# Modulation of the opening computed in quarters instead of halves, in a transformer block kernel on Trainium2

## The chip, the cores and the metric

The kernel runs on one core of a Trainium2 chip. Its engines work side by side, each through its own list of instructions in order: TensorE (PE, matrix products and transpositions), VectorE (DVE), ScalarE (ACT), GpSimd (POOL) and SyncE (SP, which here only issues transfers). The metric is the time of one execution on the device in microseconds; 3 runs are known of the kernel before.

## The reference

One layer of a diffusion transformer over 2048 tokens of width 1024, with 256 context tokens. What the opening of the kernel has to do with:

```
mod_x = silu(c) @ w_mod + b_mod            # six vectors of 1024; the first two: shift sh1, scale sc1
mod_c = silu(c_ctx) @ w_mod + b_mod        # the same for the context tokens
h_x = rmsnorm(x, norm1_g) * (1 + sc1) + sh1
h_c = rmsnorm(ctx, norm1_g) * (1 + sc1c) + sh1c
p_x = h_x @ w_in                           # columns: k | v | q | u | vg | gate a | gate b
k_c, v_c = (h_c @ w_in[:, :256]) split     # keys and values of the context
... attention, gated mixing, branch merge, residual
... second norm, squared-ReLU MLP, residual
```

Everything is float32.

## The kernel before

`project` computes the input projection for two blocks of 1024 tokens. Each is a 2 x 2 block product (tokens in halves of 512, the inner width in halves of 512, columns in halves) done with seven products instead of eight. They come in the order `SUMS = (0, 1, 5, 6, 4, 2, 3)`. Product 0 has as its left operand `h[0]`, the first token half with inner half 0; product 1 has `h[1]`, the first token half with inner half 1. Products 5, 6, 4 have sums and differences that need the second token half (`x1` in the code) as well. `h_five` makes the operand of product 5 from the turned pieces of both halves.

A product has two chunks `c`, each of two 128-row pieces of the inner width. A float32 product is done as three matmuls of a faster format: each operand is split into a high part (a cast on ACT) and a low part (a subtraction on DVE), and `product` multiplies high by high, high by low, low by high (lines 1744, 1745, 1746). A chunk of the first pair of columns thus has 4 token tiles x 2 pieces x 3 = 24 matmuls of 384 columns. `pair_chunk` casts and splits the weights of one chunk (lines 712, 713); `ready` holds the chunks that are prepared.

The left operands must stand with the inner width on the partitions. So `turn` transposes four 128 x 128 tiles on PE (line 192, in `transposes`), and one ACT instruction (line 537) applies the modulation's scale `G1` and shift `S1` on the way out of PSUM. `operand` casts and splits the result (lines 572, 573). `h_scale` squares and sums x on ACT (line 515), takes the reciprocal root in small DVE steps (lines 163 to 179) and scales x on DVE (line 524).

`G1` and `S1` come from the modulation, which is done in halves of 512 columns (four pieces of 128). `mod_weights` loads 16 tiles of w_mod of 256 KB each; `mod_products` multiplies them with the silu of the two conditioning vectors, 32 columns wide (line 339); `mod_finish` copies the row out (line 348), transposes it (line 351) and adds bias and norm weight on DVE (lines 357, 361). The first half is done in `mod_head` before any product, the second by the generator `opening` between products 0 and 1.

`opening` is a generator with the work that goes between the products: `pairs_run` calls its hook twice a chunk, and each call runs `opening` to its next `yield`. It turns x1 (`raw_turned`), prepares product 5's operands and, with `opening_terms`, the weights of products 5, 6, 4 and 3. Those of 4 and 3 go to DRAM (`t_d`) and are loaded back for their product. From the hook's 20th call on (`CONTEXT_AT`) it runs `context_keys`, which turns the context tokens (line 999) and multiplies them.

The order of each engine comes from the framework's scheduler, within limits that the kernel writes down: for index ranges in `pins` the order written holds on all engines, in `fixed` on PE and DVE, in `loads` on SP. Each queue, those of DMA issues too, is worked through in order. PSUM has 4 banks named "a" for the products and 4 named "b" for all else.

Of the kernel before, what the change touches and what calls it, by code (L numbers as in the profile page):

```python
# [13 lines left out]
ALU = mybir.AluOpType  # L14
# [4 lines left out]
P = 128  # L19
D = 1024  # L20
KC = D // P
# [5 lines left out]
GROUPS = 8  # L27
# [40 lines left out]
CONTEXT_AT = 20  # L68
ON_VECTOR = (2, 4, 8, 14)
# [3 lines left out]
class Kern:  # L73
# [115 lines left out]

    def transposes(self, ps, srcs):  # L190
        for i, s in enumerate(srcs):
            self.nc.tensor.transpose(ps[:, i * P : (i + 1) * P], s, self.ident)  # L192
# [88 lines left out]
    def mod_head(self):  # L281
# [4 lines left out]
        at = 0  # L286
        for src, eng in (
            (I["c"][0], nc.sync),
            (I["c_ctx"], nc.sync),
            (I["b_mod"][0, : 2 * D], nc.scalar),  # L290
            (I["norm1_g"][0], nc.scalar),
        ):
            src = src.rearrange("(k p) -> k p", p=P)
            eng.dma_start(rows[at : at + src.shape[0]], src)
            at += src.shape[0]
        nc.scalar.dma_start(rows[at : at + GROUPS], I["gm_bs"][0])
        self.rope_consts()
        at += GROUPS
# [20 lines left out]
        w = self.mod_weights(0, "hx")  # L319
        self.h_scale(self.x0, dve=True)  # L320
        ps = self.bank([TB])
        for k in range(KC):
            self.mod_products(ps, w, k)
        self.mod_finish(ps, 0)

    def mod_weights(self, half, tag):
        w = []
        for k in range(KC):
            w.append([self.sb(tag, [TB]) for _ in range(2)])
            for i, t in enumerate(w[k]):  # L330
                lo = i * D + half * TB
                self.nc.sync.dma_start(
                    t, self.I["w_mod"][0, k * P : (k + 1) * P, lo : lo + TB]
                )
        return w

    def mod_products(self, ps, w, k):
        for i in range(2):
            self.nc.tensor.matmul(
                ps[32 * i : 32 * i + 32], self.wide[:, k, :], w[k][i],  # L340
                start=k == 0, stop=k == KC - 1,
            )

    def mod_finish(self, ps, half):
        nc = self.nc
        bcol, gcol = self.mod_cols
        row = self.t2([TB])
        nc.scalar.copy(row[:64], ps[:64])
        pt = self.bank([HK, 64])
        for j in range(HK):  # L350
# [3 lines left out]
        ks = slice(half * HK, (half + 1) * HK)  # L354
        for i, dst in enumerate((self.S1, self.G1)):
            bs = slice(i * KC + half * HK, i * KC + (half + 1) * HK)
            nc.vector.tensor_tensor(
                out=dst[:, ks], in0=pt[:, :, 32 * i : 32 * i + 2],
                in1=bcol[:, bs].unsqueeze(2).broadcast_to([P, HK, 2]), op=ALU.add,
# [3 lines left out]
            in1=gcol[:, ks].unsqueeze(2).broadcast_to([P, HK, 2]),  # L363
# [352 lines left out]
    def pairs_run(self, pairs, h, ready, hook, direct):  # L716
# [246 lines left out]
    def context_keys(self):  # L963
# [8 lines left out]
        for k0 in range(0, KC + 2, 2):  # L972
# [19 lines left out]
            if k0 < KC:  # L992
# [3 lines left out]
                tmp = self.t2([2, CTX])  # L996
                for j in range(2):
# [114 lines left out]
    def project(self, tail):  # L1112
# [15 lines left out]
        for kk in range(HK):  # L1128
            t = raw[0, kk] = self.m4([2, TB])
            self.turn(self.x0, kk, t[:, 0])  # L1130
            if kk % 2 == 0:
                ready.append(self.pair_chunk(pairs[0], 0, kk // 2, loaded[kk // 2]))
            h[0].append(self.operand(0, t[:, 0]))
        self.h_scale(x1, dve=True)

        def opening(raw=raw, h=h):
            for _ in range(4):
                yield
# [1296 lines left out]
```

## Time and profile before

| what | value |
|---|---|
| runs shown | 3006.05, 3006.0 and 3002.89 us, median 3006.0 |
| profiled execution | 3006.42 us, its span 3004.3 us |
| PE busy | 2929.0 us, 97% of the span |
| DVE busy | 2073.7 us, 69% |
| ACT busy | 1418.8 us, 47% |
| PE busy in the first 100 us | 78.6 us |
| PE busy from 100 to 120 us | 12.19 us of 20 |
| granted TensorE clock over the span | 0.992 |

Times in the rows are microseconds from the start of the span. A row of the timeline gives start, length, engine, line, operation, what is written from what, and shapes; in brackets stands how long the engine sat idle before it, and what ended that. A matmul's length contains its way through the array; what it costs in a series is the distance between two starts.

### The profile page before, as it was taken

To read this page: it belongs to the slowest core of one execution; us is meant where nothing else is said; L and a number is where in the kernel's file an instruction comes from. 1 tells how busy PE (TensorE), PEld (TensorE's weight loads), DVE (VectorE), ACT (ScalarE), POOL (GpSimd) and SP (SyncE) were. 2 spreads that over 40 slices of the span, in tenths; PEclk is the share of its full clock that TensorE was granted. 3 is DMA by queue.
4 is the path that set the end of the run, shared out by engine and by line. 5 is a ranking of instruction groups with operands and counts; after the bars stand their busy time and mean duration, and the time that the engine had idled before them with its cause. 6 is when DMAs were issued, how large, how long until landed. Compare 5 with 4: busy or idle time off the path is not lost.

```text
span 3004.3 us, 37936 instructions
## 1 busy us (share of the span) xinstructions
PE 2929.0 (97%) x13325; PEld 2211.2 (74%) x13325; DVE 2073.7 (69%) x2983; ACT 1418.8 (47%) x2318; POOL 654.0 (22%) x470
## 2 busy tenths in 40 slices
PE   7899999999999999999999989999999999999999
PEld 5778788876555555556888878888887888888887
DVE  4857487766888898777555588776676766654555
ACT  5645765554454454544222354444454344444432
POOL 0000000001999899894121200000000000000000
PEclk9999999999999999999999999999999999999999
DMA  7687966775010010016776659888766544447654
GB/s 269 190 288 258 313 211 215 255 250 163 24 36 29 22 37 22 22 43 193 232 218 188 189 194 320 306 302 306 262 218 221 182 152 155 154 164 267 210 210 154
DMA packets 386175, 559.04 MB, mean 186 GB/s; under 512 B 38640, under 2 KB 192416, under 8 KB 385984
## 3 DMA queue, kind: packets, MB, share of 16 engines
q1 hardware_dynamic: 373616, 535.89, 53.7%
q10 hardware_dynamic: 12368, 20.73, 1.8%
q8 instruction: 105, 1.72, 0.2%
q14 instruction: 86, 0.70, 0.1%
HBM read 379.75 MB, written 176.69 MB: 185 GB/s over the span
## 4 chain that ended last, share of the span: by engine, by line
PE 82%; DMA 7%; DVE 7%; ACT 2%; issue 2%; SPq 0%; POOL 0%; DVEq 0%; ACTq 0%; POOLq 0%
PE b L1744 14%; PE b L1745 14%; PE b L1746 14%; PE b L2322 9%; PE b L2291 5%; PE b L2310 4%; PE b L186 4%; PE b L187 4%; PE b L188 4%; PE b L2246 3%; PE a L1744 2%; PE a L1745 2%; PE a L1746 2%; PE b L192 1%; DMA m<-ws_d 1%
## 5 line engine op out<-in xcount | busy, mean ns | idle before, releaser
L2257 DVE TENSOR_REDUCE ts<-b 128x1 f32<-128x512 f32 x492 | 301.8, 681 | 66.9 <-PE b L2246 66.9
L2342 POOL TENSOR_TENSOR ac<-ac,p 128x512 f32<-128x512 f32 x214 | 313.6, 1498 | 48.3 <-ACT p L2314 48.3
L1860 DVE TENSOR_TENSOR b<-b,b 128x1024 fp32r<-128x1024 f32 x170 | 200.7, 1220 | 136.5 <-ACT b L1859 136.1
L1859 ACT CAST b<-b 128x1024 fp32r<-128x1024 f32 x170 | 170.7, 1051 | 226.1 <-PE b L1746 100.1
L2314 ACT ACTIVATE p<-b 128x512 f32<-128x512 f32 x384 | 193.8, 627 | 168.3 <-PE b L2310 160.6
L1745 PE MATMUL b<-b,b 128*128 128x512 f32 x680 | 265.1, 390 | 3.5 <-DVE b L1860 3.5
L1744 PE MATMUL b<-b,b 128*128 128x512 f32 x680 | 266.2, 391 | 2.3 <-DVE f L1881 1.4
L1746 PE MATMUL b<-b,b 128*128 128x512 f32 x680 | 264.7, 389 | 0.0
L2342 POOL TENSOR_TENSOR ac<-p,p 128x512 f32<-128x512 f32 x32 | 52.8, 1667 | 742.1 <-ACT p L2314 742.1
L2342 POOL TENSOR_TENSOR ac<-ac,t 128x512 f32<-128x512 f32 x152 | 198.9, 1337 | 0.0
L2291 PE MATMUL b<-h,h 128*128 128x512 f32 x576 | 187.0, 405 | 3.3 <-ACT p L2314 2.0
L2322 PE MATMUL b<-p,h 128*64 128x512 f32 x768 | 186.9, 610 | 0.0
L2310 PE MATMUL b<-h,h 128*128 128x512 f32 x576 | 178.6, 391 | 0.0
L1745 PE MATMUL b<-hb,b 128*128 128x512 f32 x446 | 173.8, 390 | 0.0
L1754 DVE TENSOR_TENSOR f<-f,b 128x512 f32<-128x512 f32 x160 | 109.1, 682 | 82.5 <-issue 47.8
L1744 PE MATMUL b<-hb,b 128*128 128x512 f32 x415 | 161.8, 390 | 0.0
L1746 PE MATMUL b<-hb,b 128*128 128x512 f32 x415 | 161.3, 389 | 0.0
L1745 PEld LDWEIGHTS b<-b,b 128*128 128x128 f32 x680 | 127.6, 188 | 31.7 <-DVE b L1860 5.0
L2291 PEld LDWEIGHTS b<-h,h 128*128 128x128 f32 x576 | 103.6, 188 | 63.9 <-DVE ts L2257 24.3
L1744 PEld LDWEIGHTS b<-b,b 128*128 128x128 f32 x680 | 127.7, 188 | 30.7 <-ACT b L1859 3.4
L1746 PEld LDWEIGHTS b<-b,b 128*128 128x128 f32 x680 | 127.6, 188 | 26.3
L1757 ACT ACTIVATE f<-f 128x512 f32<-128x512 f32 x96 | 60.5, 630 | 141.7 <-DVE f L1754 141.7
(440 smaller groups left out, 7260.8 us busy)
## 6 DMA issues: line engine op xcount, KB each, us to landing
ao_d<-f SPq DMA_DIRECT2D x224, 256.0 KB
f<-in_w_ff SPq DMA_DIRECT2D x48, 1024.0 KB
b<-ao_d SPq DMA_DIRECT2D x85, 512.0 KB
b<-w2o_d SPq DMA_DIRECT2D x85, 512.0 KB
w2o_d<-f SPq DMA_DIRECT2D x112, 256.0 KB
f<-in_w_in SPq DMA_DIRECT2D x38, 512.0 KB
f<-x_d SPq DMA_DIRECT2D x64, 256.0 KB
hb<-ao_d SPq DMA_DIRECT2D x54, 256.0 KB
```

The costliest lines, as they stand in the source:

```text
L186: mm(ps, sh, mh, start=start, stop=False)
L1744: mm(ps, wh, hh, start=start and k == 0, stop=False, skip_group_check=True)
L1745: mm(ps, wh, hl, start=False, stop=False, skip_group_check=True)
L1746: mm(ps, wl, hh, start=False, stop=k == len(w) - 1, skip_group_check=True)
L1859: nc.scalar.copy(h, f32(l))
L1860: nc.vector.tensor_tensor(out=l, in0=f32(l), in1=f32(h), op=ALU.subtract)
L2257: nc.vector.tensor_reduce(out=self.mx[:, t, h, c : c + 1], in_=ps[h], axis=AX.X, op=ALU.max)
L2291: self.nc.tensor.matmul(self.pts[j][h], k.KA[c][self.kv][:, ks], self.qa[h], start=True, stop=False, skip_group_check=True,)
L2310: self.nc.tensor.matmul(s, k.KB[c][self.kv][:, ks], self.qb[h], start=False, stop=True, skip_group_check=True,)
L2314: self.nc.scalar.activation(pt[h], s, AF.Exp)
L2322: nc.tensor.matmul(self.o[h * HD : (h + 1) * HD, :], k.V[c][:, i, self.kv * HD : (self.kv + 1) * HD], pt[h], start=j == 0, stop=j == NKT - 1,)
L2342: nc.gpsimd.tensor_tensor(out=self.acc[e][:, h], in0=old[:, h], in1=pt[h], op=ALU.add)
```

## The change

The modulation is done in four quarters of 256 columns (`MQ = 2` pieces of 128). Its weights are re-packed on the host, so that a quarter's tile for one inner piece (shift and scale columns side by side) is one contiguous block of 256 KB; a quarter is eight such tiles. Conditioning, bias, norm weight and gm_bs come in one array, in one load instead of five.

`project` now loads, in this order: a chunk of product weights, quarter 0, a chunk, quarter 1, a chunk, quarter 2, x1, a chunk, quarter 3, then the terms' weights. Quarter 0 is finished before product 0; quarter 1's products go into product 0's first chunk, and so on; quarter 3 comes between product 1's chunks. `h_scale(x1)` moves behind the third quarter's turns. x1's four groups of transpositions come one chunk later. `fill` adds multiplications of the constant `ones` with the identity, whose results nobody reads: 28 before quarter 0's products, 3 between its tiles, 14 before every second turn of a quarter, 16 before quarter 3's products, and 36 before the context's first transposition. Read-ahead of weight chunks is 1 up to step 5 and 3 behind it; before it grew from 1 to 3 at steps 3 to 5.

```diff
+    def fill(self, ps, n):
+        at = self.here()
+        for _ in range(n):
+            self.nc.tensor.matmul(ps[:, :P], self.ones, self.ident, start=True, stop=True)
+        self.fixed.append(range(at, self.here()))
...
+    def mod_weights(self, q, tag):
         w = []
         for k in range(KC):
-            w.append([self.sb(tag, [TB]) for _ in range(2)])
-            for i, t in enumerate(w[k]):
-                lo = i * D + half * TB
...
+            t = self.sb(tag, [2, MQ * P])
+            self.nc.sync.dma_start(t.rearrange("p i c -> p (i c)"), self.I["w_mod1"][q, k])
+            w.append(t)
+        return w
+
+    def mod_row(self, w, ahead=0, between=0):
+        nc = self.nc
+        pt = self.bank([TB])
+        ps = self.bank([MQ * P])
+        self.fill(pt, ahead)
+        for k in range(KC):
+            if k:
+                self.fill(pt, between)
+            for i in range(2):
+                nc.tensor.matmul(
+                    ps[32 * i : 32 * i + 32], self.wide[:, k, :], w[k][:, i],
+                    start=k == 0, stop=k == KC - 1,
                 )
...
+        row = self.t2([MQ * P])
+        nc.scalar.copy(row[:64], ps[:64])
+        return row, pt
...
-    def turn(self, xs, k, out):
+    def turn(self, xs, k, out, fill=0):
         ps = self.bank([TB])
+        self.fill(ps, fill)
         self.transposes(ps, [self.columns(x, k) for x in xs])
...
-            depth = 3 if direct is None else min(3, max(1, at - 2))
+            depth = 3 if direct is None or at > 5 else 1
...
+                if k0 == 0:
+                    self.fill(ps.rearrange("p j c -> p (j c)"), 36)
...
-        loaded = [self.pair_load(pairs[0], 0, c) for c in range(2)]
-        x1 = self.x_load(self.x_block(1), TT, lambda n: self.sb("hx", n), 2)
-        wm = self.mod_weights(1, "h")
-        loaded += [self.pair_load(pairs[0], 1, c) for c in range(2)]
+        wm, loaded = [], []
+        for q in range(4):
+            if q == 3:
+                x1 = self.x_load(self.x_block(1), TT, lambda n: self.sb("hx", n), 2)
+            loaded.append(self.pair_load(pairs[0], q // 2, q % 2))
+            wm.append(self.mod_weights(q, "h" if q > 1 else "hx"))
...
+        def quarter(q, raw=raw, h=h):
+            j, c = q // 2, q % 2
+            for kk in (2 * c, 2 * c + 1):
+                if not j:
+                    raw[0, kk] = self.m4([2, TB])
+                t = raw[0, kk][:, j]
+                self.turn(self.x0, kk + j * HK, t, 14 * (kk % 2))
+                h[j].append(self.operand(j, t))
+
+        chunk(0)
+        self.mod_finish(*self.mod_row(wm[0], 28, 3), 0)
+        quarter(0)
 
         def opening(raw=raw, h=h):
-            for _ in range(4):
-                yield
...
+            yield
+            chunk(1)
+            row = self.mod_row(wm[1])
+            yield
+            self.mod_finish(*row, 1)
+            quarter(1)
+            yield
+            chunk(2)
+            row = self.mod_row(wm[2])
+            yield
+            self.mod_finish(*row, 2)
+            quarter(2)
+            self.h_scale(x1, dve=True)
+            yield
+            chunk(3)
+            yield
+            self.mod_finish(*self.mod_row(wm[3], 16), 3)
+            quarter(3)
+            next(terms)
             yield
             turned = self.raw_turned(1, x1, raw, self.t4)
```

Three places of the built order. First SP, ahead of the first products: f is a chunk of product weights, hx a tile of w_mod or a half tile of x1, t a tile of x0. Before:

```order
L332 DMA hx_447<-in_w_mod 128x512
L332 DMA hx_450<-in_w_mod 128x512
L332 DMA hx_451<-in_w_mod 128x512
L694 DMA f_40_510<-in_w_in 128x2x384
L694 DMA f_42_513<-in_w_in 128x2x384
L505 DMA hx_516<-in_x 128x512
L505 DMA hx_517<-in_x 128x512
```

After, from the last tile of x0:

```order
L502 DMA t_11_416<-in_x 128x1024
L692 DMA f_21_447<-in_w_in 128x2x384
L322 DMA hx_450<-in_w_mod 128x512
L322 DMA hx_452<-in_w_mod 128x512
L322 DMA hx_454<-in_w_mod 128x512
L322 DMA hx_456<-in_w_mod 128x512
L322 DMA hx_458<-in_w_mod 128x512
L322 DMA hx_460<-in_w_mod 128x512
L322 DMA hx_462<-in_w_mod 128x512
L322 DMA hx_464<-in_w_mod 128x512
L692 DMA f_31_466<-in_w_in 128x2x384
L322 DMA hx_469<-in_w_mod 128x512
```

A chunk of weights and eight tiles now stand between x0 and the first quarter's end, where 16 tiles stood before the first chunk.

Second PE, at the last of x1's four groups of transpositions (`<-ident,hx`). a is a product's bank; f_145 and f_71 are weights of product 1, f_151 and, in the kernel after, f_164 and f_165 are weights of product 5. Before:

```order
L1746 MATMUL a_697<-f_145_828,h_825 128x384
L192 MATMUL b_967<-ident,hx_516 128x128
L192 MATMUL b_967<-ident,hx_520 128x128
L192 MATMUL b_967<-ident,hx_524 128x128
L192 MATMUL b_967<-ident,hx_528 128x128
L192 MATMUL b_973<-ident,hx_517 128x128
L192 MATMUL b_973<-ident,hx_521 128x128
L192 MATMUL b_973<-ident,hx_525 128x128
L192 MATMUL b_973<-ident,hx_529 128x128
L1744 MATMUL a_694<-f_151_860,h_894 128x384
```

After (f_185 belongs to product 5's second chunk):

```order
L1762 MATMUL a_687<-f_164_1088,h_1105 128x384
L199 MATMUL b_1161<-ident,hx_504 128x128
L199 MATMUL b_1161<-ident,hx_508 128x128
L199 MATMUL b_1161<-ident,hx_512 128x128
L199 MATMUL b_1161<-ident,hx_516 128x128
L199 MATMUL b_1167<-ident,hx_505 128x128
L199 MATMUL b_1167<-ident,hx_509 128x128
L199 MATMUL b_1167<-ident,hx_513 128x128
L199 MATMUL b_1167<-ident,hx_517 128x128
L1760 MATMUL a_684<-f_185_1173,h_1144 128x384
```

The group stood between products 1 and 5; it now stands between the two chunks of product 5.

Third ACT, around x1's first turned pieces (`ACTIVATE t<-b,S,G`), the high parts of product 5's first weights (f), the high part of its first operand (h), and results that leave (t from a, p_d) or are put back (a from t). Before:

```order
L537 ACTIVATE t_148_847<-b_848,S_74,G_73 128x512
L537 ACTIVATE t_148_847<-b_854,S_74,G_73 128x512
L631 CAST f_151_860<-hx_806 128x384
L631 CAST f_151_860<-hx_833 128x384
L537 ACTIVATE t_153_878<-b_879,S_74,G_73 128x512
L537 ACTIVATE t_153_878<-b_885,S_74,G_73 128x512
L572 CAST h_894<-t_156_891 128x512
L2125 COPY t_159_904<-a_694 128x384
```

After:

```order
L535 ACTIVATE t_154_1038<-b_1039,S_74,G_73 128x512
L535 ACTIVATE t_154_1038<-b_1045,S_74,G_73 128x512
L2141 COPY t_159_1061<-a_686 128x384
L2145 DMA p_d_0_129<-t_159_1061 128x384
L725 COPY a_686<-t_115_778 128x384
L2141 COPY t_160_1071<-a_687 128x384
L2145 DMA p_d_0_129<-t_160_1071 128x384
L725 COPY a_687<-t_116_779 128x384
L535 ACTIVATE t_161_1075<-b_1076,S_74,G_73 128x512
L535 ACTIVATE t_161_1075<-b_1082,S_74,G_73 128x512
L629 CAST f_164_1088<-hx_1016 128x384
L629 CAST f_164_1088<-hx_1053 128x384
```

Two leaving results now stand between the two pairs of turned pieces, and the weights' casts behind both pairs.

More of the change, by code (lines that the diff above doesn't have):

```diff
@@ L68 @@
 CONTEXT_AT = 20
+MQ = 2
 ON_VECTOR = (2, 4, 8, 14)
@@ L285, in mod_head @@
         rows = self.t2([P])
[L286 to L296, printed above, removed]
+        at = I["head"].shape[0]
+        nc.sync.dma_start(rows[:at], I["head"])
         self.rope_consts()
-        at += GROUPS
         cols = self.bank([at])
@@ L1127, in project, with chunk @@
         at = self.here()
[L1128 to L1134, printed above, removed]
[L1136 to L1149 removed]
+        def chunk(q):
+            ready.append(self.pair_chunk(pairs[0], q // 2, q % 2, loaded[q]))
+        def quarter(q, raw=raw, h=h):
[9 more added lines that the diff above has]
+        quarter(0)
+        def opening(raw=raw, h=h):
+            yield
[17 more added lines that the diff above has]
+            next(terms)
             yield
```

64 lines of the change are left out of this document (21 added, 43 removed).

## The prediction

> **What bounds the kernel now.** I read the totals first, then stretches of the opening, then its single instructions.
>
> ```profile
> PE 2929.0 (97%) x13325; PEld 2211.2 (74%) x13325; DVE 2073.7 (69%) x2983; ACT 1418.8 (47%) x2318; POOL 654.0 (22%) x470
> ```
>
> TensorE (PE) is busy for 97% of the span, and nothing in the program is tied to a fixed time: what PE loses or gains in the opening moves all that follows. So the change is worth the shift of the opening's end. Stretches next; columns: stretch, length, busy us and count of PE, PEld, DVE, ACT, POOL, then granted clock, DMA share, GB/s. The last two show PE alone.
>
> ```profile
> 10.00:20.00 10.00, 8.13 (x25) 2.43 (x26) 4.71 (x16) 2.04 (x4) 0.00 (x0) 1.00 1.05 393
> 40.00:50.00 10.00, 7.54 (x46) 3.21 (x40) 3.42 (x11) 3.49 (x6) 0.00 (x0) 1.00 1.01 343
> 80.00:90.00 10.00, 9.99 (x58) 9.65 (x57) 10.00 (x18) 7.19 (x13) 0.00 (x0) 1.00 0.52 159
> ...
> 29.00:31.00 2.00, 2.00 (x7) 0.50 1.05 386
> 53.00:55.00 2.00, 2.00 (x9) 0.50 0.47 170
> ```
>
> Until about 50 us the DMA engines are full (share 1.0). From 80 us VectorE (DVE) is busy without a break. Twice PE runs at half the granted clock. The same as a timeline of PE (start, length, line, tiles, count, wait in brackets):
>
> ```profile
> 11.87 11.12 PE L339 MATMUL b<-hx,t 128*32 128x512 f32 x32 [6.25 <-DMA hx<-in_w_mod]
> 24.05 1.97 PE L192 MATMUL b<-ident,t 128*128 128x128 f32 x16
> 26.81 0.45 PE L1744 MATMUL a<-f,h 128*128 128x384 f32 x1 [0.80 <-ACT h L572]
> 29.67 0.52 PE L1745 MATMUL a<-f,h 128*128 128x384 f32 x1
> 29.99 0.52 PE L1746 MATMUL a<-f,h 128*128 128x384 f32 x1
> 37.51 0.33 PE L1744 MATMUL a<-f,h 128*128 128x384 f32 x1
> 37.68 0.33 PE L1745 MATMUL a<-f,h 128*128 128x384 f32 x1
> 38.12 7.06 PE L339 MATMUL b<-h,t 128*32 128x512 f32 x32
> 50.57 0.44 PE L1744 MATMUL a<-f,h 128*128 128x384 f32 x1 [2.27 <-ACT f L712]
> 54.27 1.91 PE L192 MATMUL b<-ident,hx 128*128 128x128 f32 x8
> 58.97 0.42 PE L1744 MATMUL a<-f,h 128*128 128x384 f32 x1
> 64.92 0.42 PE L1744 MATMUL a<-f,h 128*128 128x384 f32 x1
> 98.51 0.33 PE L1744 MATMUL a<-f,hx 128*128 128x384 f32 x1
> 106.66 0.34 PE L1746 MATMUL a<-f,hx 128*128 128x384 f32 x1
> 116.45 0.69 PE L1744 MATMUL a<-f,hx 128*128 128x384 f32 x1 [1.09 <-ACT a L734]
> ```
>
> With SUMS = 0,1,5,6,4,2,3 and two chunks of 24 matmuls for each product, the starts are: product 0 at 26.81, its second operand half (product 1) after 38.12 to 45.18 of modulation at 50.57 and 58.97, product 5 at 64.92, product 2 at 98.51, and after 9.5 us without a product, product 3 at 116.45. A matmul costs 37.68 - 37.51 = 0.17 us at full clock (0.173 over a longer run) and 0.32 at half (29.99 - 29.67).
>
> **The change part by part.**
>
> *The first product starts earlier.* In the rows below: ACT has x0's last tile at 11.10; a 256 KB tile lands each 0.69 us.
>
> ```profile
> 11.10 1.06 ACT L515 ACTIVATE t<-t 128x1024 bf16<-128x1024 f32 x1 [0.20 <-DMA t<-in_x]
> 19.20 0.14 PEld L339 LDWEIGHTS b<-hx,t 128*32 128x32 f32 x2 [0.53 <-DMA hx<-in_w_mod]
> 19.89 0.14 PEld L339 LDWEIGHTS b<-hx,t 128*32 128x32 f32 x2 [0.55 <-DMA hx<-in_w_mod]
> 25.42 0.82 ACT L712 CAST f<-f 128x768 fp32r<-128x768 f32 x1
> ```
>
> Now one 384 KB chunk (1.0 us) and eight tiles (5.5) stand behind x0: 17.6, and 0.4 for the last pair: 18.0, where the last of 32 passes ended at 22.99. From there to the first product took 26.81 - 22.99 = 3.8, 0.8 of it the chunk's cast, which now is done before: 21.0, so 5.8 us earlier. One load for five small ones, which frees ACT's queue of three and SP's of one, is worth 0 to 0.4 us, since x0 bounds; I take 0. The re-packed weights are as many tiles of 256 KB in rows of the same 2 KB, so I keep 0.69 for each. Read-ahead of one chunk instead of two or three at product 5's steps moves no load that PE waits for there (its weights come from x-independent terms), so nothing; if it did, it would add to the late case.
>
> *A quarter costs PE a cycle.* The modulation's products cost the same in all (7.06 us for a half, 3.5 for a quarter), and the second set of small operations that each half's split adds (a row copy, two transpositions, three on DVE) lies in the 2.7 below. A constant multiplication is not in this trace: a 512-column pass takes 7.06/32 = 0.22, so two passes of 128 columns 0.11; the upper bound is 0.22, if a pass never goes below what a transposition takes (1.97/16 = 0.12, doubled). I take 0.11, as columns set the pass everywhere else. The three between tiles (0.33) with a pair (0.44) then just fill the 0.69 a tile needs; the 28 ahead of them end before 11.9.
> Per chunk: 24 matmuls 4.2; products of the next quarter 3.5; the transposition of its row, four of x0, 14 constants, four more: 0.2 + 0.45 + 1.55 + 0.45 = 2.7, in which ACT's turn and cast are hidden; and the first six matmuls wait for the second operand (26.81 to 29.67 went into seven matmuls worth 1.2; the clock took 0.15, the wait about 1.3, which I take). Sum 11.7. So product 0's second chunk starts at 32.7, product 1's first at 44.4, and it ends at 44.4 + 4.2 + 1.3 = 49.9. DMA, at 0.69 a tile, has long delivered these quarters, so PE no longer waits for weights.
>
> *The fourth quarter* follows: 16 constants 1.8, products 3.5: 55.2. But x1 is now scaled right ahead of it on ACT and DVE, behind the third quarter's turns.
>
> ```profile
> 31.25 0.62 ACT L515 ACTIVATE t<-hx 128x512 bf16<-128x512 f32 x1
> 36.29 0.16 DVE L517 TENSOR_TENSOR ts<-ts 128x4 f32<-128x4 f32 x1 [4.22 <-ACT t L515]
> 38.87 3.26 DVE L524 TENSOR_SCALAR hx<-hx,ts 128x512 f32<-128x512 f32 x8
> 55.36 1.63 ACT L537 ACTIVATE t<-b,S,G 128x512 f32<-128x512 f32 x2 [1.45 <-PE b L192]
> 56.90 0.91 ACT L631 CAST f<-hx 128x384 fp32r<-128x384 f32 x2
> 58.37 0.68 DVE L583 TENSOR_TENSOR m<-m,t 128x512 f32<-128x512 f32 x1
> 60.67 0.48 ACT L2125 COPY t<-a 128x384 f32<-128x384 f32 x1
> 63.28 1.45 ACT L537 ACTIVATE t<-b,S,G 128x512 f32<-128x512 f32 x2
> 65.26 0.69 DVE L573 TENSOR_TENSOR h<-t,h 128x512 fp32r<-128x512 f32 x1 [2.43 <-ACT h L572]
> 73.72 0.69 DVE L573 TENSOR_TENSOR h<-t,h 128x512 fp32r<-128x512 f32 x1 [0.68 <-ACT h L572]
> 99.79 0.55 DVE L2127 TENSOR_TENSOR t<-t,a 128x384 f32<-128x384 f32 x1
> 101.21 1.05 SPq L710 DMA_DIRECT2D f<-t_d x1
> ```
>
> Squares 8 x 0.62 from 45.9: 50.8. DVE then needs 38.87 + 3.26 - 36.29 = 5.8: 56.6, a chunk's low part 0.9, three small operations 0.5: 58.0, and a turn and cast on ACT 1.4. Product 1's second chunk starts at 59.4, against 58.97: the 5.8 us are used up. The two half-clock stretches that disappear (11 matmuls x 0.15 = 1.6 us each) are in this, since I priced all at 0.17.
>
> *x1's transpositions come one chunk later.* Before, their four groups stood inside product 1's two chunks (54.27 the first) and ended ahead of product 5; now the last two stand inside product 5, whose own operands wait for the first two. From 59.4: half a chunk with its wait 3.4, a group 0.9, half a chunk 2.1, a group 0.9: 66.7. On ACT four copies and stores (63.28 - 60.67 = 2.6) stand ahead of each turned pair (1.45), and the cast of the weights (0.9) now behind the second pair: 61.8 + 2.6 + 1.5 + 2.6 + 1.4 + 0.9 = 70.8. DVE has the low part of these weights ahead of the sums (+0.4), then twice two sums (1.4), ACT's cast (0.6), a low part (0.7): 76.6. Before, the same operand's low part was done at 65.95. Then half of product 5's first chunk 1.2, a group 0.9, the other half 2.1, a group 0.9: 81.7; pair 1.4, casts 0.9, low part 0.4, sums 1.4, cast 0.6, low part 0.7: 87.1, against 73.72 + 0.69 = 74.4. That is +12.7.
>
> *What is got back.* Before, DVE bounded what followed: from 74.4 to product 2 at 98.5 passed 24.1 us for 96 matmuls worth 16.6. Now DVE's order lets product 6 go on after eight mixed operations and two low parts (5.3: 92.4), and 92 matmuls (15.9) follow: product 2 at 108.3. The wait and half clock at 91 to 97 are gone. Shift +9.8.
>
> *Product 3* waits for its weights, loaded back from DRAM behind the leaving results (DVE 99.79, issue 101.21), so it moves along; the 36 constants (4 us) lie in this wait of 116.45 - 106.99 = 9.5 us. The 17 matmuls now behind the first context transposition lie in it too. I leave +9.8, less 0.2 for the warmer restart: **+9.6**. Against the profiled execution's 3006.42 (span 3004.3, 2.1 around it) that is 3016.0; the median of the runs shown, 3006.0, is its like.
>
> The Trainium skill, "TensorE: Matmul & The Clock Gate", Part 1, says that PE's clock is halved after an idle window of about 3.4 us and comes back after a busy one. The 0.50 rows above, behind 2.27 us of wait in a thin stretch, agree in kind. By this rule the constants earn the 3.2 us already counted, but PE's idle 7 us ahead of product 5, where no constants stand, would halve the clock there: some 1.6 more, 3017.6.
>
> **The rivals.**
> *The early start is kept.* ACT and DVE keep up (DVE is busy for only 3.4 of 10 us at 40 to 50), product 5 has its operands, and 5.8 + 3.2 us stay: 2997. For it speaks the room on DVE; against it that each queue runs in order and x1's turns stand behind product 5's start. It decides if product 5's last operand is done before 68 (74.4 - 6).
> *The wait ahead of product 3 takes it in.* If its weights come as early as before, PE's 9.5 us of idleness shrink by what product 2 lost: 3006, and a change that does nothing. The load's place behind the leaving stores speaks against it; the two gate loads in its way now go one store earlier, which speaks for a part.
>
> **How the numbers follow.** A difference of 0.2% (6 us) is about what a measurement tells from none: faster is below 3000, slower above 3012. The late x1 chain 0.58, 3008 to 3024 (above 3012 in 0.53); the kept start 0.20, 2994 to 3002 (below 3000 in 0.17); the wait that takes it in 0.22, 3003 to 3012. Faster 0.17, same 0.30, slower 0.53. The high end has constants at 0.22: 4 x 1.5 + 1.8 on the path less what waits hide, some +7. The low end takes in most of the kept start: 2997 to 3023; the likeliest case alone 3010 to 3023.
>
> **What would show it.** First product near 21 us; product 1's second chunk near 59; x1's second transposition group near 66; several us of PE waiting for ACT's cast ahead of product 5, at about 67 to 73; product 2 near 108 and product 3 near 126. I am wrong if product 5 starts before 66 with no wait, if chunks cost 9 us, or if product 3 starts near 116 all the same.

## The result, and the profile after

The changed kernel takes 3042.86 us (median of 4 runs, 3039.25 to 3047.77), the kernel before 3006.03 (4 runs): a ratio of 1.0121, 95% interval 1.0106 to 1.0135, so 36.8 us more. Slower was forecast, but by 9.6 us.

Totals of the changed kernel, then four stretches of it (columns as in the prediction):

```profile
PE 2965.2 (97%) x13703; PEld 2247.6 (74%) x13703; DVE 2074.3 (68%) x2989; ACT 1419.4 (47%) x2320; POOL 654.1 (21%) x470
...
10.00:20.00 10.00, 9.15 (x70) 6.45 (x69) 5.58 (x17) 3.25 (x7) 0.00 (x0) 1.00 1.06 389
40.00:50.00 10.00, 8.90 (x72) 6.44 (x70) 2.34 (x3) 3.96 (x7) 0.00 (x0) 1.00 1.04 348
80.00:90.00 10.00, 3.41 (x22) 3.12 (x20) 2.86 (x5) 6.40 (x12) 0.00 (x0) 0.89 0.33 117
90.00:100.00 10.00, 8.71 (x36) 7.75 (x35) 6.12 (x11) 2.79 (x4) 0.00 (x0) 0.60 0.22 79
```

The share of PE is the same 97%, its busy time 36.2 us longer. From 80 to 90 us, where VectorE had no break before, PE is busy for 3.41 us of 10 and VectorE for 2.86, and the clock falls behind it to 0.60. PE's timeline (lines 1760 to 1762 are the products, 335 the modulation's, 194 the constant multiplications):

```profile
3.21 9.40 PE L194 MATMUL b<-ident,ones 128*128 128x128 f32 x56
...
13.46 0.63 PE L335 MATMUL b<-hx,t 128*32 128x256 f32 x4 [0.85 <-DVE ts L171]
14.02 0.94 PE L194 MATMUL b<-ident,ones 128*128 128x128 f32 x6
...
28.74 0.42 PE L1760 MATMUL a<-f,h 128*128 128x384 f32 x1
...
32.66 3.65 PE L335 MATMUL b<-hx,t 128*32 128x256 f32 x32
39.28 3.29 PE L194 MATMUL b<-ident,ones 128*128 128x128 f32 x28
42.41 0.60 PE L199 MATMUL b<-ident,t 128*128 128x128 f32 x4
42.76 0.42 PE L1760 MATMUL a<-f,h 128*128 128x384 f32 x1
...
56.79 0.42 PE L1760 MATMUL a<-f,h 128*128 128x384 f32 x1
62.68 3.73 PE L194 MATMUL b<-ident,ones 128*128 128x128 f32 x32
75.06 0.42 PE L1760 MATMUL a<-f,h 128*128 128x384 f32 x1
89.48 0.69 PE L1760 MATMUL a<-f,h 128*128 128x384 f32 x1 [6.59 <-ACT h L570]
...
127.81 0.33 PE L1760 MATMUL a<-f,hx 128*128 128x384 f32 x1
132.98 8.20 PE L194 MATMUL b<-ident,ones 128*128 128x128 f32 x72
147.05 0.44 PE L1760 MATMUL a<-f,hx 128*128 128x384 f32 x1 [0.35 <-ACT a L732]
```

A constant multiplication appears as two passes, so x28 are fourteen: from 39.28 to the next start at 42.41, 3.13/28 = 0.112 us a pass and 0.224 for one. A tile of the first quarter takes 14.02 - 13.46 plus its six passes, 1.42 us, and the first product comes 1.9 us later than before instead of 5.8 earlier. A chunk takes 42.76 - 28.74 = 14.0 us.

VectorE and ScalarE ahead of product 5:

```profile
84.56 1.44 ACT L535 ACTIVATE t<-b,S,G 128x512 f32<-128x512 f32 x2
85.89 0.91 ACT L629 CAST f<-hx 128x384 fp32r<-128x384 f32 x2
...
86.42 1.03 DVE L631 TENSOR_TENSOR f<-hx,f 128x384 fp32r<-128x384 f32 x2 [6.80 <-ACT f L629]
92.17 0.69 DVE L571 TENSOR_TENSOR h<-t,h 128x512 fp32r<-128x512 f32 x1 [0.68 <-ACT h L570]
105.18 0.69 DVE L571 TENSOR_TENSOR h<-t,h 128x512 fp32r<-128x512 f32 x1 [0.68 <-ACT h L570]
```

The first chunk's operand for product 5 is done at 92.9 (65.95 before), the last at 105.9 (74.4).

Where the time came from is seen by landmarks. The last column but one is ScalarE's first copy of a gate step, behind product 3's restart; first before, then after:

```profile
138.52 0.59 ACT L2182 COPY b<-t 128x512 f32<-128x512 f32 x1
...
167.04 0.59 ACT L2198 COPY b<-t 128x512 f32<-128x512 f32 x1
```

The landmarks are each of one profiled execution, the medians of all.

| kernel | first product | product 1, chunk 2 | product 5 | product 2 | gate copy | median, less before's in the same series |
|---|---|---|---|---|---|---|
| before | 26.8 | 59.0 | 64.9 | 98.5 | 138.5 | |
| changed | 28.7 | 75.1 | 89.5 | 127.8 | 167.0 | +36.8 |
| no constants | 22.3 | 60.8 | 75.6 | 114.8 | 155.7 | +23.2 |
| no constants, first quarter | 24.2 | 70.5 | 84.9 | 123.2 | 162.1 | +25.6 |
| no constants, turns and fourth quarter | 26.9 | 68.5 | 83.3 | 122.4 | 161.2 | +24.2 |
| no constants, context | 28.5 | 74.8 | 89.3 | 127.5 | 168.0 | +37.2 |
| narrow constants | 26.4 | 73.3 | 87.7 | 126.3 | 168.6 | +35.7 |
| none, sums first | 21.7 | 63.3 | 78.3 | 114.6 | 156.8 | +22.3 |
| none, x1's turns early | 22.2 | 60.6 | 73.5 | 110.3 | 151.8 | +24.3 |
| none, all of x1 early | 21.5 | 61.7 | 73.7 | 110.9 | 153.3 | +18.9 |
| none, x1 and terms early | 21.7 | 61.4 | 69.3 | 108.3 | 146.9 | +12.1 |
| none, order as before | 21.5 | 63.5 | 70.9 | 107.2 | 146.8 | +8.0 |

The medians spread by some 5 us from run to run, the landmarks by a few. At the gate copy the changed kernel is 28.5 us late; the other 8 come in behind it. In the profiled run 5.3 of them arise at about 700 us, where PE waits for a load (waits of PE from 600 to 760 us: us in all, times, longest), against 1.2 for the longest of these waits before:

```profile
PE b L187 <- DMA m<-ws_d: 7.5, 4, 4.3
```

The run without the context's constants, as late at the gate copy, has no such step. Four others lose 5.1 to 6.3 us at 780 to 800 us instead (no constants; narrow constants; x1's turns early; x1 and terms early). Only these four have the following wait there, and half clock for 3.4 to 6.8 us close behind it:

```profile
PE b L2260 <- ACT p L2328: 2.0, 1, 2.0
```

So a step of some 5 us comes in single executions, and a median can differ by that from what its landmarks say. What sets it off, no run was made to show.

### The profile page after: what moved, and what is told of

Same layout as the page of the kernel before. It is cut to its first block, busy times and chain, and to the rows that moved or that the text cites. A ratio compares the mean times of both kernels' runs of the same rounds, so it can differ in the third digit from the quotient of the medians.

```text
span 3042.7 us, 38691 instructions
## 1 busy us (share of the span) xinstructions
PE 2965.2 (97%) x13703; PEld 2247.6 (74%) x13703; DVE 2074.3 (68%) x2989; ACT 1419.4 (47%) x2320; POOL 654.1 (21%) x470
## 5 line engine op out<-in xcount | busy, mean ns | idle before, releaser
L2307 PEld LDWEIGHTS b<-h,h 128*128 128x128 f32 x576 | 103.4, 188 | 63.9 <-DVE ts L2273 24.3
L1760 PE MATMUL a<-f,h 128*128 128x384 f32 (+1 forms) x320 | 118.6, 375 | 18.2 <-ACT h L570 13.2
```

Source lines behind the costliest of these rows:

```text
L1760: mm(ps, wh, hh, start=start and k == 0, stop=False, skip_group_check=True)
L2307: self.nc.tensor.matmul(self.pts[j][h], k.KA[c][self.kv][:, ks], self.qa[h], start=True, stop=False, skip_group_check=True,)
```

## The experiments

**Constant multiplications out, all and by place.** All:

```diff
-            self.mod_finish(*self.mod_row(wm[0], 28, 3), 0)
+            self.mod_finish(*self.mod_row(wm[0]), 0)
-            self.turn(self.x0, kk + j * HK, t, 14 * (kk % 2))
+            self.turn(self.x0, kk + j * HK, t)
-            self.mod_finish(*self.mod_row(wm[3], 16), 3)
+            self.mod_finish(*self.mod_row(wm[3]), 3)
-                if k0 == 0:
-                    self.fill(ps.rearrange("p j c -> p (j c)"), 36)
```

> All constant multiplications are left out (the 28 and 3 of the first quarter, the 14 in front of every second turn, the 16 ahead of the fourth quarter, the 36 ahead of the context); the rest of the change stays. Theory A (the constant multiplications are the cost: 0.224 us each, twice the price of the prediction, so they reach past the waits that they were meant to fill): the first product goes from 28.7 to about 23, a chunk of products from 14.0 us to about 12, product 5 from 89.5 to about 73, and the time from 3042.9 to about 3021. Theory B (they lie in waits that are there anyway; the cost is the cut in quarters with x1's turns one chunk later): the time stays at 3038 to 3043, and the chunk keeps 13 us or more, since what the constant multiplications did is then idle. Theory C (they keep the clock up, and without them TensorE falls to half clock ahead of every chunk): matmuls of 0.32 us instead of 0.17 in the four chunks, 3.5 us more for each, and the time rises above 3043.

Its timeline of PE (the last row is VectorE's, the last operand for product 5):

```profile
13.37 6.04 PE L335 MATMUL b<-hx,t 128*32 128x256 f32 x32 [10.03 <-DVE ts L171]
...
22.31 0.44 PE L1758 MATMUL a<-f,h 128*128 128x384 f32 x1 [1.08 <-ACT h L570]
34.10 0.45 PE L1758 MATMUL a<-f,h 128*128 128x384 f32 x1 [1.08 <-ACT h L570]
45.91 0.44 PE L1758 MATMUL a<-f,h 128*128 128x384 f32 x1 [1.08 <-ACT h L570]
60.75 0.69 PE L1758 MATMUL a<-f,h 128*128 128x384 f32 x1 [3.45 <-ACT h L570]
75.60 0.69 PE L1758 MATMUL a<-f,h 128*128 128x384 f32 x1 [5.96 <-ACT h L570]
114.75 0.33 PE L1758 MATMUL a<-f,hx 128*128 128x384 f32 x1
...
90.81 0.69 DVE L571 TENSOR_TENSOR h<-t,h 128x512 fp32r<-128x512 f32 x1 [0.68 <-ACT h L570]
```

3030.65 us, ratio 1.008 (1.0055 to 1.0104). The tiles go at 6.04/8 = 0.75 us. The loads set that only in part: up to 18 us the pairs of passes start 0.43 us apart, behind that 0.22, so PE goes at half its own pace most of the time. A chunk takes 34.10 - 22.31 = 11.8 us instead of 14.0; product 2 comes 13.1 us earlier. B, by which the constants lie in waits, is refuted for the quarters. But 17 us of lateness remain: A's landmarks came within 3 us, its time of 3021 did not. C is refuted up to product 1's second chunk (the granted clock is 1.00 from 20 to 50 us), but it names a real trade: up to the gate copy the clock is at half for 30.7 us here and for 10.2 us with the constants (20.5 in the kernel before). The constants did hold the clock; they cost more than that was worth.

The edits by place are single lines of the diff above. First quarter (28 and 3):

> Only the 28 constant multiplications ahead of the first quarter and the 3 between its tiles are left out. Theory A: between tiles of the first quarter 1.42 us become the pace of the loads, some 0.7 to 1.0 us, the first product comes at 22 to 24 instead of 28.7, and the time falls by 5 to 6 us to about 3037. Theory B (the loads set the pace of the first quarter): the last tile comes no earlier than now, the first product stays within 1.5 us of 28.7, and the time within 2 us of 3043.

3033.09 us, ratio 1.0091 (1.0065 to 1.0116): 4.6 us at the first product, the same 4.5 at product 5. A holds at the landmarks. The median fell by 11.2 us, twice what A says, but only 4.9 of that stand at the gate copy.

Turns and fourth quarter (14 and 16):

> Only the 14 in front of every second turn and the 16 ahead of the fourth quarter are left out. Theory A: every second operand is cast about 2.1 us earlier (turn and cast of the first take 1.4 us on ScalarE, and 3.29 us of constant multiplications stand there now), four times 2.1 and the 3.7 of the sixteen are 12 us, so about 3031. Theory B: TensorE waits for ScalarE's casts and the row copy in the same places, and the time stays within 3 us of 3043. Theory C (clock): matmuls of 0.32 us appear in the chunks and the time rises.

3031.66 us, ratio 1.0081 (1.0056 to 1.0107). 6.2 us at product 5, not 12: a chunk took 40.24 - 26.88 = 13.4 us, the granted clock from 20 to 50 us being 0.89 instead of 1.00 (the last section comes back to it). A in sign, half in size; with theory C in it. That the time came out near A's 3031 is luck: at the gate copy 5.8 us are gained, not 12.

Context (36):

> Only the 36 ahead of the context's transpositions are left out (8.2 us on TensorE in the trace of the changed kernel, inside product 2). If they lie in the wait for ScalarE's scaling of the context that the kernel before shows with 5.45 us: TensorE waits instead, product 3 goes on at most 2 us earlier, and the time stays within 2.5 us of 3043. If they push product 2's second half and with it the context: up to 8 us less, 3035.

3044.72 us, ratio 1.0127 (1.01 to 1.0154): nothing. Eight microseconds of constants replace a wait there, as the prediction had it.

**What sets the price of a pass.** First 32 weight columns instead of 128:

```diff
-            self.nc.tensor.matmul(ps[:, :P], self.ones, self.ident, start=True, stop=True)
+            self.nc.tensor.matmul(ps[:32, :P], self.ones[:, :32], self.ident, start=True, stop=True)
```

> The changed kernel with all its constant multiplications, each with 32 columns of ones as weights instead of 128; the moving matrix stays at 128 columns. Theory P1 (a pass takes what its weights take to load, 0.112 us for 128 columns, more than its own 128 columns): the pass falls to about 0.06 us, fourteen of them from 3.29 us to 1.6, the first quarter's tiles from 1.42 us to about 1.0, the first product from 28.7 to about 25, product 5 from 89.5 to about 81, and the time to about 3034. Theory P2 (a pass of 128 float32 columns takes 0.11 us whatever its weights): all stays where it is, 3043 within 4 us.

3041.03 us, ratio 1.0109 (1.0093 to 1.0125), and fourteen still took as long:

```profile
22.80 3.25 PE L194 MATMUL b<-ident,ones 128*32 128x128 f32 x28
```

P1 is refuted as the sole cause. (Only between the first quarter's tiles did it help, 1.42 to 1.09 us a tile; that was not followed further.) So shapes were set by place, in two kernels with one profiled run each:

```diff
+    SHAPES = [(P, P, P), (P, 32, P), (32, 32, P), (P, 64, P), (P, P, 32), (64, P, P), (P, 256, P)]
...
+            self.nc.tensor.matmul(ps[:m, :c], self.ones[:k, :m], mv, start=True, stop=True)
```

> The changed kernel, its constant multiplications in other shapes by place, to price a pass: ahead of the first quarter 128 weight columns, 128 moving columns, 128 rows as now; in front of the second turn of quarter 0 128 weight columns and 32 moving, of quarter 1 32 and 32, of quarter 2 128 and 64, of quarter 3 64 and 128; the sixteen 128 and 128 with 32 rows; ahead of the context 128 and 256. The run with narrow weights kept 0.116 us a pass, so theory P2a says: a pass of up to 256 moving columns has a floor of about 0.11 us whatever its shape (fourteen constant multiplications 3.1 to 3.3 us in all four places, the 36 still about 8.2 us). Theory P2b (the moving columns set it, 128 of them at the 0.11 us that a pass shows now): 0.03 us with 32 columns (fourteen in 0.8 us), 0.06 with 64 (1.6 us), 0.22 with 256 (36 in 16 us).

Timeline of PE in that kernel; the last row is the end of the 36, which were split by a product (shapes: rows * weight columns, then rows x moving columns):

```profile
25.00 3.88 PE L201 MATMUL b<-ident,ones 128*128 128x32 f32 x28
42.78 1.07 PE L201 MATMUL b<-ident,ones 128*32 128x32 f32 x28
54.74 3.24 PE L201 MATMUL b<-ident,ones 128*128 128x64 f32 x28
...
74.94 3.27 PE L201 MATMUL b<-ident,ones 128*64 128x128 f32 x28
139.68 13.11 PE L201 MATMUL b<-ident,ones 128*128 128x256 f32 x60
```

Neither P2a nor P2b. Per pass: 64 moving columns with 128 of weights 0.116; 128 moving with 64 of weights 0.117; 32 and 32 0.038; 256 and 128 0.219 (row lengths over counts; the last pass's way through the array is in them). In the first row the clock fell on the way; the last section has it. Both sides cost 0.11 us for 128 columns, and the longer counts. Narrowing one alone gains nothing. The Trainium skill, "TensorE: Matmul & The Clock Gate", section "LDWEIGHTS (loading the stationary operand)", gives a weight load as its columns over 1.2 in ns, 107 ns for 128; the row with 64 moving columns, 0.116 us a pass, agrees to within 8%.

That leaves the modulation's passes, from which the prediction took its price: 512 moving columns and 0.22 us in the kernel before, 256 and 3.65/32 = 0.114 in the changed one, half as much per column as here. They are written in pairs to different output rows.

```diff
+    SHAPES = [(P, P, 1), (32, 256, 1), (32, 256, 2), (32, P, 2), (P, P, 1), (32, P, 1), (P, 32, 1)]
...
+            lo = 32 * (i % g)
+            self.nc.tensor.matmul(ps[lo : lo + m, :c], self.ones[:, :m], mv, start=True, stop=True)
```

> The changed kernel, its constant multiplications in other shapes by place, to see why the modulation's passes looked half as dear per column as these: those are written in pairs, one to output rows 0 to 31 and one to 32 to 63. In front of the second turn of quarter 0: 32 weight columns, 256 moving, all to rows 0 to 31; of quarter 1: the same, in turn to rows 0 to 31 and 32 to 63; of quarter 2: 32 and 128, in turn; of quarter 3: 32 and 128, all to rows 0 to 31; the sixteen 128 and 128 as now; ahead of the context 128 and 32. Theory S (two multiplications with 32 weight columns run side by side when they write different rows; a single one streams 128 float32 columns in 0.11 us): fourteen take 6.1 us in quarter 0 (28 passes of 0.22), 3.2 in quarter 1, 1.6 in quarter 2 and 3.2 in quarter 3. Theory N (32 weight columns are cheap by themselves): quarters 0 and 1 both take 3.2 us and quarter 2 as much as quarter 3. The 36 with 32 moving columns: 0.11 us a pass and 8 us in all, if the weights' load of 128 columns sets them, and under 5 us if not.

```profile
25.09 6.23 PE L202 MATMUL b<-ident,ones 128*32 128x256 f32 x28
42.31 3.22 PE L202 MATMUL b<-ident,ones 128*32 128x256 f32 x28
56.53 1.72 PE L202 MATMUL b<-ident,ones 128*32 128x128 f32 x28
73.50 3.24 PE L202 MATMUL b<-ident,ones 128*32 128x128 f32 x28
```

S, in all four: the same instructions take 6.23 us into one set of rows and 3.22 in turn into two. Two narrow multiplications run side by side, in nearly half the time. Of the 36 with 32 moving columns, the first 42 passes took 4.77 us, 0.11 each, as the weights' load has it; the rest ran at a lower clock.

**What holds product 5.** From here on all are without constants. The sums ahead of the terms:

```diff
             next(turned)
-            next(terms)
             self.h_five(raw, h, 0)
             self.h_five(raw, h, 1)
+            next(terms)
...
```

> The changed kernel without constant multiplications, and in the three steps after x1's groups the sums for product 5 stand ahead of the difference terms instead of behind them (nothing else moves). In the run without constant multiplications VectorE sits idle for 7.7 us ahead of product 5, its next instruction being the low half of a term that waits for a cast which ScalarE has behind x1's second group. Theory A1 (this order holds product 5): the sums start as soon as the first group is turned, product 5 starts about 2.8 us earlier (75.6 to about 72.8), and the time falls by some 3 us to 3027. Theory A2 (x1's groups themselves are late, the order only uses up the wait): product 5 moves by less than 1 us and the time stays at 3029 to 3032.

3027.61 us, ratio 1.0074 (1.0057 to 1.009). From product 1's second chunk to product 5 took 15.0 us (14.9 without the edit). A1 is refuted: PE then waited 6.2 us for the term's cast instead of the operand's. Both are late. (The time is A1's number, but less the kernel before in its own series it is +22.3 against +23.2.)

x1's groups half a chunk earlier:

```diff
             quarter(3)
-            next(terms)
-            yield
             turned = self.raw_turned(1, x1, raw, self.t4)
             next(turned)
             next(terms)
...
```

> Without constant multiplications, x1's four groups are turned half a chunk earlier each (the first right behind the fourth quarter's turns, as close as the kernel before has them), the sums for product 5 one at a time behind each. Theory A (what is left of the loss, some 17 us at product 3, is x1's chain): product 5 starts at 66 to 69 instead of 75.6, the stretch from product 5 to product 2 shrinks from 39 to 34 us, product 2 starts at 100 to 103, and the time falls to 3010 to 3019. Theory D (the rest of the loss lies elsewhere: in the quarters, or in loads and spills behind product 2): product 5 may move but product 3 keeps its place within 4 us of 134, and the time stays above 3025.

3029.59 us, ratio 1.0072 (1.0058 to 1.0087). Product 5 came 2.1 us earlier, where 7 to 10 were expected, the gate copy 3.9; the medians, with their spread, did not show it. By its time this is D, and by its landmarks A at less than half its size.

Then x1's squares behind the second quarter, its scaling behind the third, and the fourth row in product 1's first chunk:

```diff
             quarter(1)
+            ss = self.h_squares(x1)
...
-            self.h_scale(x1, dve=True)
+            self.h_scaled(x1, ss)
             yield
             chunk(3)
+            row = self.mod_row(wm[3])
             yield
-            self.mod_finish(*self.mod_row(wm[3]), 3)
+            self.mod_finish(*row, 3)
```

> As the run before this one, and besides: x1's squares go to ScalarE behind the second quarter, its scaling to VectorE behind the third (both a half chunk or more earlier), and the fourth quarter's row is summed in the middle of product 1's first chunk, as the other rows are. Theory A: product 1's second chunk starts at about 57.7 instead of 60.8, product 5 at 63 to 66, product 2 at 96 to 100 (before: 98.5), and the time is 3002 to 3012, level with the kernel before. If the early squares get in the way of the third quarter's turns (ScalarE busy 35 to 41 us, when x1 may not have landed), product 1's first chunk comes 2 to 5 us later than 45.9, and the time is 3008 to 3016. Theory D: above 3022.

3024.25 us, ratio 1.0057 (1.0043 to 1.0071). By its time this is D again: none of A's landmarks was reached (product 5 at 73.7 instead of 63 to 66). D puts the rest of the loss elsewhere, in the quarters or behind product 2; PE's timeline names a nearer wait, twice; L651 is the cast of a term:

```profile
73.72 0.69 PE L1782 MATMUL a<-f,h 128*128 128x384 f32 x1 [4.61 <-ACT f L651]
85.82 1.33 PE L1782 MATMUL a<-f,h 128*128 128x384 f32 x3 [4.53 <-ACT f L651]
```

The terms too stood two half chunks later than before. Two steps of them moved up:

```diff
             chunk(3)
             row = self.mod_row(wm[3])
+            next(terms)
+            next(terms)
             yield
...
```

> The run with x1 early throughout, and besides the first two difference terms stand a half chunk and more earlier, behind the fourth quarter's row, so that the splits for product 5 come two half chunks earlier, as in the kernel before. Theory E (what is left is the order of the terms: product 5 waited 4.6 us for ScalarE's cast of a term and its second chunk 4.5 us for the next): the second wait goes, product 5 starts at 71 to 73 instead of 73.7, product 2 at 104 to 107 instead of 110.9, and the time falls from 3024 to 3017 to 3020. Theory F (x1's sums end just as late, the term was only the last of two): the starts stay within 2 us and the time at 3022 to 3026.

3022.98 us against 3010.92 in the same series, ratio 1.0036 (1.0024 to 1.0047). The kernel before was 5.6 us slower in this series than in the last, so the difference counts: 18.9 became 12.1, though the two intervals overlap. Both waits for a term's cast are gone, product 5 starts at 69.3, the gate copy comes 6.4 us earlier. But the operand's cast is nearly as late, which is F's point, and PE waits for it some 5 us on:

```profile
74.15 0.69 PE L1784 MATMUL a<-f,h 128*128 128x384 f32 x1 [3.66 <-ACT h L592]
```

So E holds in part: product 2 gained 2.6 us instead of 4 to 7.

At last x1's groups a further half chunk earlier, so that all stands where the kernel before has it:

```diff
+            turned = self.raw_turned(1, x1, raw, self.t4)
+            next(turned)
             next(terms)
             next(terms)
             yield
             self.mod_finish(*row, 3)
             quarter(3)
-            turned = self.raw_turned(1, x1, raw, self.t4)
             next(turned)
             next(terms)
+            self.h_five(raw, h, 0)
...
```

> As the run with the terms early, and each of x1's groups another half chunk earlier, so that x1's turns, the sums and the terms stand by the half chunks of products where the kernel before has them; left of the change are quarters, re-packed loads and x1's load ahead of the last quarter. Theory A with E (the order of x1's chain and of the terms was the whole loss behind product 1): product 5 at 66 to 68, product 2 at 99 to 102, product 3 behind the context within 5 us of 116.5, and the time 3006 to 3013. Theory G (four trips row, turn, operand cost by themselves, and the gain at the first product is used up by then): the first product stays some 4.5 us ahead of before, but product 1's second chunk comes 2 to 3 us later than before's 58.97, and all behind it keeps at least that. If neither: above 3015.

```profile
21.49 0.45 PE L1782 MATMUL a<-f,h 128*128 128x384 f32 x1 [1.08 <-ACT h L592]
34.54 0.45 PE L1782 MATMUL a<-f,h 128*128 128x384 f32 x1 [1.08 <-ACT h L592]
47.88 0.44 PE L1782 MATMUL a<-f,h 128*128 128x384 f32 x1 [1.08 <-ACT h L592]
63.54 0.44 PE L1782 MATMUL a<-f,h 128*128 128x384 f32 x1 [0.66 <-ACT h L592]
...
146.81 0.59 ACT L2220 COPY b<-t 128x512 f32<-128x512 f32 x1
```

3018.9 us against 3010.92, ratio 1.0026 (1.0016 to 1.0036). The last step brought nothing at the gate copy (146.8 against 146.9), and product 5 came at 70.9 instead of 66 to 68: A with E does not hold to the end. G holds in kind: 5.3 us ahead at the first product, 4.6 behind at product 1's second chunk (G had 2 to 3), 42.0 us for what took 32.2 before. Not all of that is trips, since this execution spent three times 3.4 us of it at half clock. No version beat the kernel before.

## Why the prediction was wrong

Right: the direction, and the chain that it rests on. Product 5 waits for ScalarE's cast (6.59 us), the early start is used up, nothing is got back ahead of product 3. With the constants out, the forecast's first landmarks are nearly met: first product 21.0 forecast, 22.3 measured; a chunk 11.7 and 11.8; product 1's second chunk 59.4 and 60.8. That is in part luck, since the forecast has the constants in it: its chunk holds 1.55 us of them, and without them PE waits for ScalarE in that place (1.08 us ahead of each of the first three chunks). The stretch from product 5's last operand to product 2 was to be 108.3 - 87.1 = 21.2 us; it was 127.8 - 105.2 - 0.7 = 21.9 in the changed kernel and 23.3 in the one without constants. Both rivals are refuted: the early start was not kept, and product 3's wait took nothing in. The shorter read-ahead, which the prediction put at nothing, is not seen to cost: between 60 and 135 us PE waits 2.0 us for the low part of a chunk's weights before, and 0.7 us after.

The step that failed is the price of a constant multiplication, "so two passes of 128 columns 0.11". It is 0.224. The row it came from is of multiplications that run in pairs side by side (6.23 against 3.22 us above), so each pass seemed half as long as it is. The forecast had 0.22 as the upper bound, from the transpositions, which are of the same shape as the constants, and took the other on the ground that columns set the pass everywhere else. The row of the same shape was the one to take.

Its effect was also counted too low, "some +7" for 0.22 instead of 0.11. With constants against without, it is 13.1 us at product 2; the two compare because the kernel without them is within 1.4 us of the forecast at product 1's second chunk, and the changed one 15.7 us late. The "+7" was added up from the fourteens and the sixteen alone, without the three between tiles. In the first quarter the three were to "just fill the 0.69 a tile needs"; at their real price a tile takes 1.42 and PE sets the pace. With the fourteen of its turn that is 28.7 - 22.3 = 6.4 us at the first product, by the runs by place 4.6 and 1.9. Each of the next two trips takes 2.2 us more, and the fourth quarter's, with its sixteen, 3.4; at product 5 13.9 of these are left.

The second term that was too small is x1's chain, +12.7: without constants it is 90.8 + 0.7 - 74.4 = 17.1. Of the 4.4 us between, 1.4 are the later start of product 1's second chunk, 1.0 come in up to the second operand (done at 79.0, forecast 76.6), and 2.2 while product 5's first chunk runs (x1's last group ends at 86.3, forecast 81.7). In both stretches the clock is at half (0.50 from 59.22 to 66.05 and from 72.87 to 83.11 us), so that a matmul takes 0.32 instead of the 0.17 that the sum has throughout. The prediction named this for product 5 beside the sum, "some 1.6 more", and did not take it in. The Trainium skill's rule as the prediction cites it, "TensorE: Matmul & The Clock Gate", Part 1, agrees in kind with the 0.60 of the changed kernel from 90 to 100 us, behind 6.59 us of waiting. The casts of the terms were in the sum (the weights' cast of 0.9 us behind the second pair). What it did not have is that they stand as late as the operand: with x1's chain alone moved up, product 5 and its second chunk waited 4.6 and 4.5 us for them.

At product 2, 108.3 was forecast and 127.8 measured. Of the 19.5 us between, 13.1 are the constants, 4.4 x1's chain and 2.0 the stretch behind it. Of the 28.5 us at the gate copy, by these single executions, the constants are 11.3 (167.0 - 155.7) and the order of x1's chain and of the terms 8.9 (155.7 - 146.8); 8.3 are left with the rest of the change: the quarters, the re-packed loads and their order. These were not taken apart. How much of the 8.3 is trips and how much half clock (its trips took 13.05 and 13.3 us, where another run had 11.8) stays open, and so does the step of some 5 us behind the gate copy.

## What to carry to other kernels

Price an added instruction by the row of its own shape and its own output rows; a row of multiplications that are written in pairs to different rows hides half of each. Work put into waits must be shorter than the wait where it stands, at its real price, or it becomes the pace. When a piece of an in-order chain is cut finer and moved, move all that feeds the same consumer with it: here the operand and the terms were both late. Moving x1's turns alone gained 3.9 us at the gate copy, the sums alone nothing, and x1 and the terms together 8.8.

## What the runs showed of the hardware

In the shapes tried, a float32 pass cost the longer of its weights' load and its moving columns, each 0.11 us for 128 columns, 0.038 for 32 and 32. Two narrow multiplications to different output rows overlapped almost fully (3.22 us against 6.23).

The same opening took 11.8 or 13.35 us for a chunk. Two kernels that do the same up to product 1's second chunk, stretches of PE (busy, granted clock, DMA share, GB/s), first the one without constants, then the one with the sums first:

```profile
20.00:35.00 15.00, 12.35 (x79) 1.00 1.06 386
```

```profile
20.00:35.00 15.00, 12.52 (x72) 0.89 1.05 385
```

The Trainium skill, "TensorE: Matmul & The Clock Gate", Part 1, says that the window by which the clock is set runs freely and starts at no program's start; waits of the same length then lower the clock in one execution and not in the next. These rows agree. So do the clock records in the traces of all 14 profiled executions: apart from the cut at the end of a record, the clock changes only at whole steps of 3.41 us, and where this grid lies against the start of the span differs. The run without constants is at half from 59.22 to 66.05 and from 72.87 to 83.11 us, the one with the sums first from 24.08 to 27.49, 37.73 to 41.15 and 61.63 to 68.45. The grid also accounts for the places not adding up: taking constants out in two places separately gave 4.5 and 6.2 us at product 5 and together 13.9, and the 3.2 us between are two chunks of 13.4 us in the run without turns' constants against 11.8 without any.

Being busy is not enough to keep the clock. In the kernel with shapes, PE was busy with 28 passes of 128 weight columns and 32 moving ones, and the clock fell during them (first row) and stayed down (second):

```profile
25.00:29.00 4.00, 4.00 (x32) 0.79 1.05 387
29.00:33.00 4.00, 3.44 (x12) 0.50 1.05 386
```

The other kernel had the same in front of the context, more clearly: its passes began at 135.44 us, PE was busy for 5.00 of 5 us from 135 to 140 and from 140 to 145, and the clock was 1.00 and then 0.60. The passes of 128 weight and 128 moving columns in that place kept 1.00 in the changed kernel. Constants that are cheap on the moving side did not hold what they were put there to hold.
